# Starting TensorE's operands at multiples of 512 bytes in a four-layer decoder trunk

## The chip, the core and the metric

The kernel runs on one core of one Trainium2 chip. The metric is the device time of one execution in microseconds (us); of several executions the median is taken.

## What is computed

A trunk of four layers on 256 tokens of width 1024, all in 32-bit floating point. Each layer is a token mixer and a multilayer perceptron (MLP), both on the RMS-normalised input, both added to it:

```
for i in range(DEPTH):
    h = _rms_norm(x, attn_norm[i])
    ...
    x = x + y.astype(x.dtype)
    hm = _rms_norm(x, mlp_norm[i])
    x = x + jnp.square(jax.nn.relu(hm @ mlp_w_up[i])) @ mlp_w_down[i]
```

The mixers `y` are, in order: sparse attention with compressed, selected and windowed keys; stick-breaking attention; a convolution module; and block attention. The MLP widens 1024 to 4096 and back. Every mixer begins and ends with a large product with a weight matrix, too.

## The kernel before

Every large product is made three times in a split form: an operand `a` is written as `hi + lo`, `hi` being `a` rounded to the type float32r, which TensorE takes in one pass, and the product is `hi*hi + hi*lo + lo*hi`. A weight tile `raw` comes from memory by a DMA of SyncE, ScalarE rounds it into `wh` (L157), VectorE writes the rest into `wl` (L158). Activations are split the same way into `xT` (normalised input), `oT` (output of a mixer) and, in the MLP, `u`.

A matrix product on TensorE has a stationary operand (at most 128 columns, loaded by a LDWEIGHTS instruction ahead of it) and a moving operand (up to 512 columns streamed through). Five groups of products make up nearly all the work:

- `dn` (L190 to L192, called for the MLP's down projection): stationary `u`, moving `wh` or `wl`, 512 columns;
- `projT` (L211, the MLP's up projection): stationary `wh` (512 columns moving) or `wl` (256), moving `xT`;
- `proj` (L190 to L192, projections of the mixers): stationary `xT`, moving `wh` or `wl`, 512 columns, some 384 or 280;
- `acc` (L218 to L220, out projections): stationary `wh` or `wl`, moving `oT`, 256 columns;
- `ab` (L917, the convolution's input projection): stationary `wh` or `wl`, moving `xT`, 256 columns.

An MLP runs eight steps j: the up projection of 512 hidden columns, their squared ReLU into `u`, and, a step behind, the down projection of the step before. A step has 64 products `projT` and 48 products `dn`. "Stages 0 to 3" below are the MLPs of the four layers; stage 1 runs inside a pool `taps` that holds tiles of the convolution to come.

Memory is given out by pools, each a run of tiles one behind the other in the order of first use, at steps of 32 bytes: `const` first (`xr`, the residual stream, then small tables), then `rawp` (three `raw`), `hlp` (eight `wh`, eight `wl`), `act` (`xT`, `oT` and helpers), `sm` (small statistics), and behind them a pool for each stage, `mlp0` with `s`, `b`, `q`, `u` for instance. So the length of an early tile sets where all later ones begin, and most tiles have lengths that are multiples of 512 bytes.

Of the kernel before, what the change touches and what calls it, by code (L numbers as in the profile page):

```python
# [10 lines left out]
F32 = mybir.dt.float32  # L11
F32R = mybir.dt.float32r
# [4 lines left out]
P = 128  # L17
# [50 lines left out]
def trunk(ctx: ExitStack, tc: tile.TileContext, A: dict, out: bass.AP):  # L68
    nc = tc.nc
    const = ctx.enter_context(tc.tile_pool(name="const", bufs=1))  # L70
    rawp = ctx.enter_context(tc.tile_pool(name="rawp", bufs=3))
    hlp = ctx.enter_context(tc.tile_pool(name="hlp", bufs=8))
    act = ctx.enter_context(tc.tile_pool(name="act", bufs=2))
    sm = ctx.enter_context(tc.tile_pool(name="sm", bufs=4))
    ps = ctx.enter_context(tc.tile_pool(name="ps", bufs=2, space=bass.MemoryType.PSUM))

    def bank(tag, name):
        return ps.tile([P, 512], F32, tag=tag, bufs=4 if tag == "B" else 2, name=name)
# [732 lines left out]
    def taps_tile(ch):  # L811


        w = tapp.tile([P, 8, 4, 32], F32, tag="taps", bufs=4, name="taps")
        nc.vector.tensor_tensor(w.rearrange("p g m (e q) -> p (g m e) q", q=16),
                                eye[:, None, :].to_broadcast([P, 64, 16]),
                                tp[:, ch, :, None].to_broadcast([P, 64, 16]), op=ALU.mult)
        taps[ch] = w
# [160 lines left out]
    def moba(n):  # L979
# [114 lines left out]
                o.go(range(4, 8), range(8))  # L1094
        return nxt

    xr = const.tile([P, KT, S], F32, name="xr")
    gains = const.tile([P, 8, KT], F32, name="gains")
    ident = const.tile([P, P], F32, name="ident")
    nc.scalar.dma_start(gains, A["norms"])  # L1100
    nc.scalar.dma_start(ident, A["ident"])
    nhalf = const.tile([P, 4], F32, name="nhalf")
    nc.vector.memset(nhalf, -0.5)
    mean = const.tile([P, P], F32, name="mean")
    nc.vector.memset(mean, 1.0 / D)
    n = start_norm(0)
    feats = list(range(KT))
# [11 lines left out]
    for _ in range(10):  # L1119
        nc.tensor.matmul(o[:, :P], lhsT=mean, rhs=mean, start=True, stop=True)  # L1120

    identr = const.tile([P, P], F32R, name="identr")
    n = nsa(n, load_x)
    n = mlp(0, n, 1)
    n = stick(n)
# [1 line left out]
    with tc.tile_pool(name="taps", bufs=1) as tapp:  # L1127
        tp = tapp.tile([P, KT, 64], F32, name="tp")
        nc.sync.dma_start(tp, A["conv_taps"])
        eye = tapp.tile([P, 16], F32, name="eye")  # L1130
        nc.sync.dma_start(eye, A["eye16"])
        n = mlp(1, n, 2, lambda j: taps_tile(j) if j < 4 else None)
        n, raw = conv(n)
# [123 lines left out]
```

## Time and profile before

| | |
|---|---|
| time, median of 3 runs | 1180.42 us (1180.06 to 1180.87) |
| profiled execution, its own time | 1180.44 us |
| its span (first to last instruction) | 1178.7 us |
| TensorE busy | 1167.1 us, 99% |
| TensorE weight loads | 1008.7 us, 86% |
| VectorE busy | 782.9 us, 66% |
| ScalarE busy | 620.9 us, 53% |
| DMA engines, share busy by hardware queue q1 | 47.0% |

TensorE's products overlap one another, so a product's duration is longer than its share of the time; the distance from the start of one to the start of the next is what counts. A weight load lies beside the product before it.

The rows of a stretch read: its limits and length in us, then busy us and count of TensorE, its weight loads, VectorE, ScalarE (and GpSimd where it appears), then TensorE's granted clock as a share of 2.4 GHz, the busy share of the DMA engines and what they moved in GB/s. Busy time there is the time covered, overlaps counted once.

### The profile page before, as it was taken

Reading aid. Unit: us, or ns where it says so; the run is one execution under the profiler, and the core shown is the slowest. Engines: PE = TensorE matmul, PEld = TensorE weight load, DVE = VectorE, ACT = ScalarE, POOL = GpSimd, SP = SyncE. Lnnn points to the kernel's source line nnn. Section 1 sums busy time; section 2 is a strip of 40 time slices with the busy share of each in tenths; the row PEclk is TensorE's granted clock in tenths of the full one; section 3 lists DMA queues with packets and bytes.
Section 4 is the critical chain, followed back from the end, with each engine's and each line's share of the span. In section 5 each row is a group of like instructions: output and inputs, shape, how many; then the busy total and the mean of one; then the engine's idle time right before and its main releaser. Section 6 shows DMA issues by size and latency. Waiting matters only on the chain.

```text
span 1178.7 us, 17661 instructions
## 1 busy us (share of the span) xinstructions
PE 1167.1 (99%) x7046; PEld 1008.7 (86%) x7046; DVE 782.9 (66%) x1206; ACT 620.9 (53%) x1031; POOL 33.2 (3%) x50
## 2 busy tenths in 40 slices
PE   9999999999999999999999999999999999999998
PEld 6798988888888998888889998888888889888886
DVE  7788675656585686656665677656659886656553
ACT  6487554444565654544563275454446665544441
POOL 1100000000000000000001100000001100000000
PEclk9999999999999999999999999999999999999999
DMA  8554255545454436545545746455455543555440
GB/s 303 203 186 144 77 210 214 185 172 204 154 201 163 144 129 222 190 183 198 188 151 165 251 172 222 164 197 212 153 195 178 182 162 118 187 214 192 165 178 36
DMA packets 35650, 211.11 MB, mean 179 GB/s; under 512 B 4592, under 2 KB 7664, under 8 KB 12016
## 3 DMA queue, kind: packets, MB, share of 16 engines
q1 hardware_dynamic: 31104, 198.76, 47.0%
q0 software_dynamic: 1568, 6.80, 2.1%
q10 hardware_dynamic: 2896, 4.42, 1.1%
q8 instruction: 55, 0.90, 0.3%
q14 instruction: 27, 0.22, 0.1%
HBM read 207.74 MB, written 2.23 MB: 178 GB/s over the span
## 4 chain that ended last, share of the span: by engine, by line
PE 67%; issue 26%; DVE 3%; ACT 2%; DMA 1%; POOL 1%; SPq 0%; POOLq 0%; ACTq 0%; DVEq 0%
PE projT L211 23%; PE dn L190 8%; PE dn L192 8%; PE dn L191 8%; PE ab L917 2%; PE proj L192 2%; PE proj L191 2%; PE proj L190 2%; PE acc L218 2%; PE acc L220 2%; PE acc L219 2%; DVE wl L158 1%; PE po L675 1%; ACT wh L157 1%; PE cv L859 1%
## 5 line engine op out<-in xcount | busy, mean ns | idle before, releaser
L158 DVE TENSOR_TENSOR wl<-raw,wh 128x1024 fp32r<-128x1024 f32 (+1 forms) x372 | 441.1, 1212 | 186.9 <-ACT wh L157 182.8
L157 ACT CAST wh<-raw 128x1024 fp32r<-128x1024 f32 (+1 forms) x372 | 376.1, 1041 | 215.6 <-PE dn L192 111.2
L211 PE MATMUL projT<-xT,wh 128*128 128x512 f32 x1152 | 361.5, 396 | 0.3 <-DVE xT L101 0.3
L211 PEld LDWEIGHTS projT<-xT,wl 128*128 128x128 f32 x1152 | 215.3, 188 | 49.9
L211 PE MATMUL projT<-xT,wl 128*128 128x256 f32 x1152 | 225.4, 278 | 0.0
L190 PE MATMUL dn<-wh,u 128*128 128x512 f32 x512 | 202.7, 396 | 0.0
L192 PE MATMUL dn<-wh,u 128*128 128x512 f32 x512 | 202.0, 395 | 0.0
L191 PE MATMUL dn<-wl,u 128*128 128x512 f32 x512 | 201.4, 393 | 0.0
L211 PEld LDWEIGHTS projT<-xT,wh 128*128 128x128 f32 x1152 | 178.2, 189 | 3.7 <-DVE xT L101 0.5
L192 PEld LDWEIGHTS dn<-wh,u 128*128 128x128 f32 x512 | 96.4, 188 | 22.4
L191 PEld LDWEIGHTS dn<-wl,u 128*128 128x128 f32 x512 | 96.4, 188 | 20.7
L190 PEld LDWEIGHTS dn<-wh,u 128*128 128x128 f32 x512 | 96.5, 188 | 20.4
L316 ACT COPY b<-projT 128x256 f32<-128x256 f32 x128 | 41.2, 374 | 93.7 <-PE projT L211 93.4
L191 PE MATMUL proj<-wl,xT 128*128 128x512 f32 (+2 forms) x224 | 85.9, 384 | 2.5 <-DVE wl L158 2.1
L190 PE MATMUL proj<-wh,xT 128*128 128x512 f32 (+2 forms) x224 | 85.7, 385 | 0.4 <-ACT wh L165 0.3
L317 DVE TENSOR_TENSOR s<-projT,b 128x256 f32<-128x256 f32 x128 | 48.2, 418 | 55.0 <-ACT b L316 55.0
L192 PE MATMUL proj<-wh,xT 128*128 128x512 f32 (+2 forms) x224 | 84.5, 378 | 0.0
L89 ACT CAST u<-q 128x1024 fp32r<-128x1024 f32 x32 | 33.6, 1049 | 82.9 <-DVE q L319 82.7
L218 PE MATMUL acc<-oT,wh 128*128 128x256 f32 x256 | 73.8, 292 | 0.0
L219 PE MATMUL acc<-oT,wh 128*128 128x256 f32 x256 | 72.7, 285 | 0.0
L220 PE MATMUL acc<-oT,wl 128*128 128x256 f32 x256 | 71.2, 284 | 0.0
L90 DVE TENSOR_TENSOR u<-q,u 128x1024 fp32r<-128x1024 f32 x32 | 39.2, 1226 | 34.5 <-ACT u L89 34.5
(231 smaller groups left out, 1252.6 us busy)
## 6 DMA issues: line engine op xcount, KB each, us to landing
raw<-in_down SPq DMA_DIRECT2D x64, 1024.0 KB, 4.8
raw<-in_up SPq DMA_DIRECT2D x63, 1024.0 KB, 4.8
raw<-in_sb_w SPq DMA_DIRECT2D x12, 1024.0 KB, 4.8
raw<-in_moba_w SPq DMA_DIRECT2D x12, 1024.0 KB, 4.9
raw<-in_conv_w SPq DMA_DIRECT2D x8, 1024.0 KB, 4.7
st<-dr POOLq DMA_DIRECT2D x16, 287.0 KB, 6.3
raw<-in_nsa_w SPq DMA_DIRECT2D x4, 1024.0 KB, 5.9
rawc<-in_nsa_cmp SPq DMA_DIRECT2D x4, 1024.0 KB, 4.8
```

The lines of the kernel that those rows point to most:

```text
L90: return a, nc.vector.tensor_sub(lo, src, hi.bitcast(F32))
L157: nc.scalar.copy(wh[:, :w], r)
L158: nc.vector.tensor_sub(wl[:, :w], r, wh[:, :w].bitcast(F32))
L190: nc.tensor.matmul(o, lhsT=aT[:, kt, 0, t, :], rhs=wh, start=first, stop=False)
L191: nc.tensor.matmul(o, lhsT=aT[:, kt, 0, t, :], rhs=wl, start=False, stop=False)
L192: nc.tensor.matmul(o, lhsT=aT[:, kt, 1, t, :], rhs=wh, start=False, stop=last)
L211: nc.tensor.matmul(o[:, :width], lhsT=v[kt][part][:, f * P:(f + 1) * P], rhs=rhs, start=kt == 0 and part == 0, stop=kt == KT - 1 and part ...
L218: nc.tensor.matmul(o, lhsT=wh, rhs=aT[:, kt, 0], start=first, stop=False, skip_group_check=True)
L219: nc.tensor.matmul(o, lhsT=wh, rhs=aT[:, kt, 1], start=False, stop=False, skip_group_check=True)
L220: nc.tensor.matmul(o, lhsT=wl, rhs=aT[:, kt, 0], start=False, stop=last, skip_group_check=True)
L316: nc.scalar.copy(b, o[:, S:])
L317: nc.vector.tensor_add(s[:, f], o[:, :S], b)
```

## The change

Tiles of the pool `const` are put in another order, and four tiles are added or widened only to fill space: `front` (384 bytes) ahead of `xr`, `nhalf` from 4 to 64 columns, `back` (384 bytes, in a pool of its own behind `sm`), and `eye` from 64 to 512 bytes, of which the first 64 are used. `front` and `back` are never read or written. The memset of `nhalf` covers its new width. No other instruction differs, and on each engine the instructions stand in the same order with the same waits.

```diff
     sm = ctx.enter_context(tc.tile_pool(name="sm", bufs=4))
+    edge = ctx.enter_context(tc.tile_pool(name="edge", bufs=1))
     ps = ctx.enter_context(tc.tile_pool(name="ps", bufs=2, space=bass.MemoryType.PSUM))
+    edge.tile([P, 96], F32, name="back")
...
+    const.tile([P, 96], F32, name="front")
     xr = const.tile([P, KT, S], F32, name="xr")
+    ident = const.tile([P, P], F32, name="ident")
+    identr = const.tile([P, P], F32R, name="identr")
+    mean = const.tile([P, P], F32, name="mean")
     gains = const.tile([P, 8, KT], F32, name="gains")
-    ident = const.tile([P, P], F32, name="ident")
...
-    nhalf = const.tile([P, 4], F32, name="nhalf")
+    nhalf = const.tile([P, 64], F32, name="nhalf")
     nc.vector.memset(nhalf, -0.5)
-    mean = const.tile([P, P], F32, name="mean")
     nc.vector.memset(mean, 1.0 / D)
...
-    identr = const.tile([P, P], F32R, name="identr")
...
-        eye = tapp.tile([P, 16], F32, name="eye")
+        eye = tapp.tile([P, P], F32, name="eye")[:, :16]
```

Where tiles begin in a partition's memory, as the remainder of the byte address by 512:

| tile | before | after |
|---|---|---|
| `xr` | 128 | 0 |
| `ident` | 384 | 0 |
| `identr`, `mean` | 416 | 0 |
| `raw`, `wh`, `wl` (all buffers) | 416 | 0 |
| `xT`, `oT` (all buffers) | 416 | 0 |
| `u` in stages 0, 2 and 3 | 32 | 0 |
| `u` in stage 1 (behind the pool `taps`) | 96 | 0 |
| `y` (stages 0 and 2; stage 1) | 32; 96 | 0; 0 |
| attention's `kT`, `vv` | 32 | 0 |
| convolution's `taps`, `st` | 96, 448 | 0, 352 |

Within `xT`, `oT` and `u`, and within `wh` and `wl` at widths of 512 and 1024 columns, every operand of a large product begins a multiple of 512 bytes behind the tile's start; at the width of 280 columns (1120 bytes) every second one does not.

## Rows read from the trace of the kernel before

**Rows 1.** The page's engine table: busy time, share of the span, instructions.

```profile
PE 1167.1 (99%) x7046; PEld 1008.7 (86%) x7046; DVE 782.9 (66%) x1206; ACT 620.9 (53%) x1031; POOL 33.2 (3%) x50
```

**Rows 2.** The page's chain that ended last, by engine and by line.

```profile
PE 67%; issue 26%; DVE 3%; ACT 2%; DMA 1%; POOL 1%; SPq 0%; POOLq 0%; ACTq 0%; DVEq 0%
```

**Rows 3.** TensorE's products by shape: count, busy us, mean ns, idle before.

```profile
L211 PE MATMUL projT<-xT,wh 128*128 128x512 f32 x1152 | 361.5, 396 | 0.3 <-DVE xT L101 0.3
L211 PE MATMUL projT<-xT,wl 128*128 128x256 f32 x1152 | 225.4, 278 | 0.0
L190 PE MATMUL dn<-wh,u 128*128 128x512 f32 x512 | 202.7, 396 | 0.0
...
L218 PE MATMUL acc<-oT,wh 128*128 128x256 f32 x256 | 73.8, 292 | 0.0
...
L190 PE MATMUL proj<-wh,xT 128*128 128x512 f32 x176 | 69.6, 398 | 0.4 <-ACT wh L165 0.3
...
L917 PE MATMUL ab<-xT,wh 128*128 128x256 f32 x256 | 47.1, 285 | 0.0
L917 PE MATMUL ab<-xT,wl 128*128 128x256 f32 x128 | 36.2, 283 | 0.0
```

**Rows 4.** Stretches with one `dn` block each, its instructions alone; stages 0, 1, 3.

```profile
186.90:198.40 11.50, 11.32 (x48) 8.90 (x48) 0.00 (x0) 0.00 (x0) 1.00 0.50 184
...
475.50:487.00 11.50, 11.16 (x48) 8.85 (x48) 0.00 (x0) 0.00 (x0) 1.00 0.51 182
...
1040.70:1052.20 11.50, 11.32 (x48) 8.94 (x48) 0.00 (x0) 0.00 (x0) 1.00 0.51 184
```

**Rows 5.** TensorE's timeline (start, duration): 47 `proj` products, first and last.

```profile
906.34 0.39 PE L191 MATMUL proj<-wl,xT 128*128 128x512 f32 x1
...
916.79 0.39 PE L192 MATMUL proj<-wh,xT 128*128 128x512 f32 x1
```

**Rows 6.** TensorE's timeline: 139 `ab` products, first and last.

```profile
629.75 0.28 PE L917 MATMUL ab<-xT,wl 128*128 128x256 f32 x1
...
646.29 0.28 PE L917 MATMUL ab<-xT,wl 128*128 128x256 f32 x1
```

**Rows 7.** A stretch that holds one step of `projT`, its instructions alone.

```profile
175.80:186.94 11.14, 11.13 (x64) 9.68 (x63) 0.76 (x2) 0.65 (x2) 1.00 0.51 188
```

**Rows 8.** Timeline of TensorE: every sixth product of 280 columns.

```profile
45.09 0.29 PE L190 MATMUL proj<-wh,xT 128*128 128x280 f32 x1
...
45.86 0.29 PE L190 MATMUL proj<-wh,xT 128*128 128x280 f32 x1
...
46.63 0.29 PE L190 MATMUL proj<-wh,xT 128*128 128x280 f32 x1
```

**Rows 9.** Timeline of TensorE: two neighbouring products of `dn`.

```profile
187.41 0.40 PE L192 MATMUL dn<-wh,u 128*128 128x512 f32 x1
187.65 0.40 PE L190 MATMUL dn<-wh,u 128*128 128x512 f32 x1
```

**Rows 10.** Two transposes' weight loads by tile: least, median, most ns; starts.

```profile
L285 PEld LDWEIGHTS xt<-ident,xr x16: 139/140/224, 1016.6 to 1019.4; 128*128 128x128 f32 x16
...
L297 PEld LDWEIGHTS yT<-ident,y x48: 138/140/143, 314.9 to 886.7; 128*128 128x128 f32 x48
```

**Rows 11.** The start: VectorE's memset by group, TensorE's timeline.

```profile
L1105 DVE MEMSET mean<- 128x128 f32 x1 | 0.2, 165 | 0.0
...
1.09 4.18 PE L1120 MATMUL warm<-mean 128*128 128x128 f32 x20 [1.09 <-DVE mean L1105]
5.56 0.73 PE L190 MATMUL proj<-wh,xT 128*128 128x512 f32 x2 [0.30 <-ACT wh L165]
```

**Rows 12.** All engines in stretches of rows 5 and 4 (stages 0, 1).

```profile
906.33:916.80 10.47, 10.47 (x48) 8.64 (x47) 10.47 (x16) 6.13 (x8) 2.01 (x2) 1.00 0.37 133
...
186.90:198.40 11.50, 11.50 (x52) 9.34 (x52) 6.38 (x7) 4.83 (x7) 0.00 (x0) 1.00 0.50 184
475.50:487.00 11.50, 11.50 (x53) 9.44 (x52) 6.51 (x8) 4.97 (x7) 0.00 (x0) 1.00 0.51 182
```

## The prediction

> **What bounds the kernel now.** The engine table comes first [rows 1]: TensorE is busy 1167.1 us of a span of 1178.7, the next engine (VectorE) 782.9. The chain of waits [rows 2] agrees: PE 67% plus "issue" 26% (time in which TensorE waited for nothing the profile shows), 3% for VectorE, 1% for DMA. So the time is the number of matrix products times the pace at which they start, and the change, which alters only where tiles lie, can reach the time through that pace alone.
>
> The pace is not the duration in the groups. There all 512-column products read 396 to 398 ns [rows 3], but neighbours overlap. The pace is read from start to start. In [rows 5] 47 products of 512 columns by `proj` start between 906.34 and 916.79: 46 intervals in 10.45 us, 227.2 ns each. In [rows 6] 139 products of 256 columns by the convolution start between 629.75 and 646.29: 138 intervals in 16.54 us, 119.9 ns each. Between them a column costs (227.2 - 119.9) / 256 = 0.419 ns, which is one column per cycle of the 2.4 GHz level (the granted clock is 1.00 in every stretch shown [rows 4]), and some 13 ns per product are left that no column pays for.
>
> The `dn` products (down projections) are slower at the same width. A block of 48 occupies 11.32 us in stages 0 and 3 and 11.16 us in stage 1 [rows 4]; less one duration of 0.395, over 47 intervals, that is 232.5 and 229.0 ns. So 5.3 and 1.8 ns above `proj`. What differs? Not what runs beside: the two stages show the same company [rows 12], VectorE 6.38 and 6.51 us of 11.50, ScalarE 4.83 and 4.97, DMA share 0.50 and 0.51; and the quicker `proj` stretch has VectorE busy all through. What does differ is the table of starts above: in `proj` both operands start at 416 within 512 bytes; in `dn` the moving one (`wh`, `wl`) starts at 416 and the stationary one (`u`) at 32 in stages 0, 2 and 3, and at 96 in stage 1. The pace follows the distance of the two starts (0, 128, 192 bytes within 512). I read this as the weight load of the next product and the stream of the running one meeting in memory, more or less often by their distance.
>
> The Trainium skill speaks against that ("TensorE: Matmul & The Clock Gate", section "Step-by-step: what each phase is for"): TensorE has two independent read ports, and loading the next weights takes nothing from the running matmul. By that rule placement would be free and the sum nothing, 1180.4 us; the two stages of [rows 4] differ all the same, so the trace does not bear it out here. No mechanism is proved by two placements, and the rule's result stays a rival.
>
> **The change part by part.**
>
> The program's instructions, their order and their waits are the same; one memset is wider, and addresses move.
>
> *The `dn` products.* `u` now starts at 0 within 512, as `wh` and `wl` do, so their distance is 0, as it always was in `proj`. If the pace follows the distance, `dn` goes to 227.2 ns: 3 stages x 384 x (232.5 - 227.2) = 6.1 us, and 384 x (229.0 - 227.2) = 0.7 us, together 6.8 us. Bounds: nothing, if distance is not the cause; and on the other side the slowest single interval that `dn` shows, 0.24 us [rows 9], as the pace of all: 1152 x (240 - 232.5) + 384 x (240 - 229.0) = 12.9 us lost. I take 227.2, since `proj` runs the same sequence (three products per weight pair, the same `wh` and `wl` buffers, a stationary tile of the same layout) at the distance that `dn` gets.
>
> *All other large products.* `projT` (weights stationary, `xT` moving), `proj`, `acc` and `ab` have both operands at 416 before and at 0 after: the distance stays 0 and only the absolute start moves. No row shows one of them at a multiple of 512 with both operands, so the price is bounded. Two rows speak for nothing. In the products of 280 columns the moving operand starts at 416 in six products and, one row of the weight tile further (1120 bytes), at 0 in the next six: starting at 45.09, 45.86 and 46.63 [rows 8], so 0.77 us for six either way, though the distance shifts with it. And the 128-column transposes load weights in a median 140 ns whether the stationary tile is `xr` (at 128, 512 bytes a slice) or `y` (at 32 or 96) [rows 10]. The bound for a gain is the whole 13 ns: 5,520 products in the groups of [rows 3] (1152 + 1152, then 3 x 512, 3 x 256, 3 x 176, 256 + 128) x 13 = 72 us. For a loss it is what a bad placement has cost `dn`, 5.3 ns on the 3,984 others: 21 us. I take 0.
>
> `projT` keeps its own small excess: 64 products in 11.13 us [rows 7], less one duration of 0.278 and over 63 intervals, is 172.2 ns, where the mean of 227.2 and 119.9 is 173.6; the last product is a short one, so it is at the level of the others within 1 ns. Nothing to win there by distance.
>
> *Other engines.* VectorE, ScalarE and the DMA queues see the same shapes at other addresses. All are covered: TensorE is the bound, and a gain of 6.8 us lowers the cover by 0.6%. If that cover failed, the next late thing would be `wl` in `dn` (VectorE, 782.9 us busy), far off.
>
> *The memset.* `nhalf` grows from 4 to 64 columns. The 128 columns of `mean` behind it take 165 ns [rows 11], so the growth costs between 0 and 0.17 us on VectorE. Behind it wait `mean` and the ten warming products, which end at 1.09 + 4.18 = 5.27 us; the first real product waits until 5.56 for ScalarE's `wh` [rows 11]. The delay is inside those 0.3 us; without that cover it would cost some 0.08 by columns. I take 0.
>
> *Sum.* The profiled execution took 1180.44 us, 0.02 above the median of the three runs, 1180.42. 1180.44 - 6.8 = 1173.6 us.
>
> **The rivals.** About 0.2% (2.4 us) is what a measurement of this kernel can tell from no change; on the 1,536 `dn` products that is 1.5 ns each, on all 5,520 0.43 ns.
>
> A, the forecast: `dn` goes to the pace of `proj`. With 227 to 231 ns reached, 1170 to 1178. For it: two placements, two paces, the same in each of the 48-product blocks [rows 4]. Chance 0.47.
>
> B, nothing moves: `dn` is slow for a reason of its own (it waits less often than `proj`, so its weight loads come at another moment), and placement only nudges it. The time stays within 1178.1 to 1182.8. Against it: `proj` has the same order. Chance 0.22.
>
> C, the absolute start matters to all products, since a start off some boundary makes the array fetch one piece more. Then the 13 ns go in part or whole: half of them on 5,520 is 36 us, which gives 1144; all 72, 1108; a tenth on top of A, 1166. The same page of the Trainium skill (section "Back-to-back issue gap") gives N / 2.4 + 2.5 ns for an isolated gap, by which 512 columns would take 215.8 and not the 227.2 measured; that leaves room for C, and no run here shows such a pace. For C: nothing large in this trace is aligned, so nothing refutes it. Against: [rows 8, 10]. Chance 0.16, 0.10 of it below 1160.
>
> D, slower: the distance of 0 suits `proj` by its walk over the tiles, not `dn`; the weight load and the stream now begin at the same place and meet at every product. Place: `dn`, in all four stages. If `dn` goes to its 0.24 us level throughout, 1180.4 + 12.9 = 1193; it decides from a mean pace of (1152 x 232.5 + 384 x 229.0) / 1536 = 231.6 ns upward, and shows as slower from 233.1. For it: single `dn` intervals at that level exist. Chance 0.15.
>
> **How the numbers follow.** The time is A's, 1173.6. Faster: A and C, 0.63; same: B, 0.22; slower: D, 0.15. The range takes A, B, the lower edge of D (up to 1184) and the part of C above 1160: 0.47 + 0.22 + 0.04 + 0.06 = 0.79. A alone is 1170 to 1178.
>
> **What would show it.** In the changed kernel's trace 48 `dn` products should occupy 0.395 + 47 x 0.2272 = 11.07 us in every stage, stage 1 no longer apart from the rest; `proj`, `ab` and `projT` should keep 227, 120 and 11.13 us. If `proj` and `ab` are quicker, C is right; if `dn` keeps 11.32 and 11.16, B; if a `dn` block takes over 11.4 us, D. The forecast is wrong if distance is not the cause, or if absolute starts count.

## The result and the profile after

The changed kernel takes 1172.55 us (median of 5, 1171.66 to 1173.2) against 1180.06 beside it: a ratio of 0.9935, 95% interval 0.9921 to 0.995. The forecast was 1173.6. The changed file is longer ahead of the products, so their lines move by two: `dn` and `proj` are now L192 to L194, `projT` L213, `acc` L220 to L222, `ab` L919.

The groups of TensorE's products by shape answer to [rows 3]:

```profile
L213 PE MATMUL projT<-xT,wh 128*128 128x512 f32 x1152 | 361.4, 396 | 0.3 <-DVE xT L103 0.3
L213 PE MATMUL projT<-xT,wl 128*128 128x256 f32 x1152 | 225.3, 278 | 0.0
L192 PE MATMUL dn<-wh,u 128*128 128x512 f32 x512 | 200.3, 391 | 0.0
```

Even in these overlapping durations `dn` alone has moved, from 396 to 391 ns. The pace shows in the stretches with one block of 48 `dn` products (its instructions alone; stages 0, 1 and 3), which answer to [rows 4]:

```profile
185.60:197.10 11.50, 11.05 (x48) 8.87 (x48) 0.00 (x0) 0.00 (x0) 1.00 0.51 184
472.30:483.80 11.50, 11.05 (x48) 8.84 (x48) 0.00 (x0) 0.00 (x0) 1.00 0.52 182
1033.90:1045.40 11.50, 11.05 (x48) 8.84 (x48) 0.00 (x0) 0.00 (x0) 1.00 0.53 184
```

All three are 11.05 us, where [rows 4] had 11.32, 11.16 and 11.32: stage 1 no longer stands apart. Less one duration of 0.39, over 47 intervals, that is 226.8 ns. Of the full blocks only the first of stages 0 to 2 is slower, before as after: its first interval takes 0.31 to 0.32 us, and it occupies 11.17 us, where before had 11.40 in stages 0 and 2 and 11.24 in stage 1. The same 47 `proj` products as in [rows 5] and the same 139 `ab` products as in [rows 6], first and last of each on TensorE's timeline:

```profile
899.82 0.39 PE L193 MATMUL proj<-wl,xT 128*128 128x512 f32 x1
...
910.27 0.39 PE L194 MATMUL proj<-wh,xT 128*128 128x512 f32 x1
```

```profile
625.78 0.28 PE L919 MATMUL ab<-xT,wl 128*128 128x256 f32 x1
...
642.32 0.28 PE L919 MATMUL ab<-xT,wl 128*128 128x256 f32 x1
```

10.45 us over 46 intervals and 16.54 over 138 are the very figures of before. So starting at a multiple of 512 bytes gave `proj` and `ab` nothing in these stretches. Added up over all `dn` products, the times from each start to the next start on TensorE fall from 356.6 to 349.7 us: 6.9 us of the 7.5 between the medians.

### The profile page after: what moved, and what is told of

Same layout as the page of the kernel before. It is cut to its first block, busy times and chain, and to the rows that moved or that the text cites. A ratio compares the mean times of both kernels' runs of the same rounds, so it can differ in the third digit from the quotient of the medians.

```text
span 1169.9 us, 17661 instructions
## 1 busy us (share of the span) xinstructions
PE 1159.5 (99%) x7046; PEld 1008.0 (86%) x7046; DVE 782.7 (67%) x1206; ACT 621.2 (53%) x1031; POOL 34.3 (3%) x50
## 4 chain that ended last, share of the span: by engine, by line
PE 67%; issue 26%; DVE 3%; ACT 2%; DMA 1%; POOL 1%; ACTq 0%; POOLq 0%; DVEq 0%
PE projT L213 23%; PE dn L192 7%; PE dn L194 7%; PE dn L193 7%; PE ab L919 2%; PE proj L194 2%; PE proj L193 2%; PE proj L192 2%; PE acc L220 2%; PE acc L222 2%; PE acc L221 2%; PE po L677 1%; DVE wl L160 1%; PE cv L861 1%; ACT wh L159 1%
## 5 line engine op out<-in xcount | busy, mean ns | idle before, releaser
L213 PE MATMUL projT<-xT,wh 128*128 128x512 f32 x1152 | 361.4, 396 | 0.3 <-DVE xT L103 0.3
L213 PEld LDWEIGHTS projT<-xT,wl 128*128 128x128 f32 x1152 | 215.2, 188 | 49.8
L213 PE MATMUL projT<-xT,wl 128*128 128x256 f32 x1152 | 225.3, 278 | 0.0
L192 PE MATMUL dn<-wh,u 128*128 128x512 f32 x512 | 200.3, 391 | 0.0
L194 PE MATMUL dn<-wh,u 128*128 128x512 f32 x512 | 199.5, 390 | 0.0
L213 PEld LDWEIGHTS projT<-xT,wh 128*128 128x128 f32 x1152 | 178.2, 189 | 3.5 <-DVE xT L103 0.5
L194 PEld LDWEIGHTS dn<-wh,u 128*128 128x128 f32 x512 | 96.1, 188 | 20.2
L192 PEld LDWEIGHTS dn<-wh,u 128*128 128x128 f32 x512 | 96.1, 188 | 18.7
L192 PE MATMUL proj<-wh,xT 128*128 128x512 f32 (+2 forms) x224 | 85.6, 384 | 0.4 <-ACT wh L167 0.4
L194 PE MATMUL proj<-wh,xT 128*128 128x512 f32 (+2 forms) x224 | 84.4, 377 | 0.0
L220 PE MATMUL acc<-oT,wh 128*128 128x256 f32 x256 | 74.0, 293 | 0.0
L222 PE MATMUL acc<-oT,wl 128*128 128x256 f32 x256 | 71.1, 284 | 0.0
```

Source lines behind the costliest of these rows:

```text
L192: nc.tensor.matmul(o, lhsT=aT[:, kt, 0, t, :], rhs=wh, start=first, stop=False)
L194: nc.tensor.matmul(o, lhsT=aT[:, kt, 1, t, :], rhs=wh, start=False, stop=last)
L213: nc.tensor.matmul(o[:, :width], lhsT=v[kt][part][:, f * P:(f + 1) * P], rhs=rhs, start=kt == 0 and part == 0, stop=kt == KT - 1 and part ...
L220: nc.tensor.matmul(o, lhsT=wh, rhs=aT[:, kt, 0], start=first, stop=False, skip_group_check=True)
L222: nc.tensor.matmul(o, lhsT=wl, rhs=aT[:, kt, 0], start=False, stop=last, skip_group_check=True)
```

## Experiments

"Distance" is the start of the stationary operand less that of the moving one. Distance theory: the pace depends on it. Absolute theory: it depends on whether an operand starts on a boundary.

**Distance against absolute start.** In the kernel before, `u` alone is moved inside a wider tile (the diff); in the second run, in the changed kernel, the same edit with 32, 48, 32 and 32 elements brings back the old distances.

```diff
-                u = mp.tile([P, 4, 2, NT, P], F32R, tag="u", name="u")
+                uw = mp.tile([P, 2048 + 128], F32R, tag="u", name="u")
+                at = (96, 80, 96, 96)[i]
+                u = uw[:, at:at + 2048].rearrange("p (f a t c) -> p f a t c", f=4, a=2, t=NT)
```

> The kernel before, with u alone moved inside a wider tile so that it begins at 416 within 512 bytes in all four stages, as the weight tiles do. Distance 0, no operand at a multiple of 512. Distance theory: a block of 48 dn products falls from 11.32 and 11.16 us to 11.06, the time to about 1173 us, as with the whole change. Absolute theory (a start on a boundary counts): nothing is on a boundary, blocks and time stay as before, 1180 us.

Measured: 1172.51 us, 0.994 (0.9928 to 0.9953) of before: the whole gain, with none of the change's lines. `dn` blocks of stages 0 and 1:

```profile
186.00:197.50 11.50, 11.05 (x48) 8.89 (x48) 0.00 (x0) 0.00 (x0) 1.00 0.50 184
472.70:484.20 11.50, 11.05 (x48) 8.91 (x48) 0.00 (x0) 0.00 (x0) 1.00 0.50 182
```

> The changed kernel, with u alone moved to 128 (stages 0, 2, 3) and 192 (stage 1) within 512 bytes, the distances to the weight tiles that the kernel before had; all else stays at multiples of 512. Distance theory: blocks of dn return to 11.32 us in stages 0, 2, 3 and 11.16 in stage 1, the time to 1180 us. Absolute theory with a boundary of 64 bytes or less: u is still on it, blocks stay at 11.06 us and the time at 1172.5; with a boundary of 128, stages 0, 2, 3 stay at 11.06 and stage 1 alone becomes slower.

Measured: 1179.03 us, 0.9997 (0.9988 to 1.0006) of before. The gain is gone, although the weight tiles start at a multiple of 512 and `u` at one of 64. `dn` blocks of stages 0 and 1 are those of [rows 4] again:

```profile
186.20:197.70 11.50, 11.32 (x48) 8.92 (x48) 0.00 (x0) 0.00 (x0) 1.00 0.50 184
474.70:486.20 11.50, 11.16 (x48) 8.91 (x48) 0.00 (x0) 0.00 (x0) 1.00 0.49 182
```

Together the two runs settle it for `dn`: distance 0 is enough, and aligned starts without it are worth nothing.

**How the pace depends on the distance.** The changed kernel, with the same edit and another distance in each stage. The third run was chosen after the first two had been read.

> The changed kernel with u at a distance of 64, 256, 320 and 384 bytes from the weight tiles in stages 0, 1, 2 and 3. Distance theory: each stage has its own pace, the same in all its blocks, between 226.9 and about 233 ns (blocks of 11.06 to 11.35 us), none quicker than at distance 0. Absolute theory: 256 bytes and 384 bytes at the pace of distance 0, 64 and 320 slower.

> The changed kernel with u at a distance of 16, 32, 160 and 448 bytes from the weight tiles in stages 0, 1, 2 and 3. Distance theory: small distances (16, 32) stay near 226.9 ns, 160 lies between the known 232.5 at 128 and 229.0 at 192, 448 near 227 to 229. Absolute theory (boundary of 64 bytes): 16, 32 and 160 slower by the same amount, 448 at 226.9.

> The changed kernel with u at a distance of 208, 224, 240 and 96 bytes from the weight tiles in stages 0 to 3. So far 0 and 256 gave 226.9 ns, 16, 32, 64, 160 and 320 gave 233.3 to 233.4, 128 and 384 gave 232.5, 192 and 448 gave 229.1: the distance counts within 256 bytes. Distance theory: 96 near 233, 208 to 240 between 229 and 233. If a distance just short of 256 lets the weight load run clear of the stream, one of 208 to 240 falls below 226.9; I expect none.

Measured, one execution each, 1179.23 and 1180.86 us; `dn` blocks of stages 0 to 3, at 64, 256, 320, 384 bytes, then at 16, 32, 160, 448:

```profile
186.00:197.60 11.60, 11.37 (x48) 8.87 (x48) 0.00 (x0) 0.00 (x0) 1.00 0.50 182
474.80:486.30 11.50, 11.05 (x48) 8.91 (x48) 0.00 (x0) 0.00 (x0) 1.00 0.49 182
748.80:760.40 11.60, 11.37 (x48) 8.89 (x48) 0.00 (x0) 0.00 (x0) 1.00 0.49 181
1039.50:1051.00 11.50, 11.31 (x48) 8.93 (x48) 0.00 (x0) 0.00 (x0) 1.00 0.51 184
```

```profile
186.60:198.20 11.60, 11.36 (x48) 8.97 (x48) 0.00 (x0) 0.00 (x0) 1.00 0.50 182
475.70:487.20 11.50, 11.36 (x48) 8.87 (x48) 0.00 (x0) 0.00 (x0) 1.00 0.50 182
751.80:763.30 11.50, 11.36 (x48) 8.87 (x48) 0.00 (x0) 0.00 (x0) 1.00 0.50 182
1042.20:1053.70 11.50, 11.16 (x48) 8.89 (x48) 0.00 (x0) 0.00 (x0) 1.00 0.50 184
```

256 equals 0, 320 equals 64, 384 equals 128 (11.31 and 11.32) and 448 equals 192: to within 0.01 us the pace repeats every 256 bytes. The absolute theory in the forms set down above fails again: 384 and 448, on boundaries of 128 and 64 bytes, are slower than 256. (With everything else at 0 these runs can't exclude a boundary of 256; the first experiment did, with `u` and the weight tiles all at 416.) My own guess that 16 and 32 bytes stay near 226.9 ns was wrong, too: 16 bytes already cost 0.31 us a block. The third run, 1180.44 us, at 208, 224, 240 (two blocks of stage 2, one in each of `u`'s two buffers) and 96:

```profile
186.20:197.70 11.50, 11.29 (x48) 8.93 (x48) 0.00 (x0) 0.00 (x0) 1.00 0.52 184
474.80:486.40 11.60, 11.36 (x48) 8.91 (x48) 0.00 (x0) 0.00 (x0) 1.00 0.50 181
751.30:762.80 11.50, 11.05 (x48) 8.90 (x48) 0.00 (x0) 0.00 (x0) 1.00 0.51 182
773.30:784.80 11.50, 11.13 (x48) 8.92 (x48) 0.00 (x0) 0.00 (x0) 1.00 0.52 182
1040.20:1051.70 11.50, 11.40 (x48) 8.89 (x48) 0.00 (x0) 0.00 (x0) 1.00 0.53 184
```

No distance beats 0, and 96 is the worst. At 240 the two buffers differ by 0.08 us, in turn from block to block, so the remainder within 256 bytes is not the whole rule.

**Do the other products depend on it?** `xT` and `oT` are moved by the same kind of edit, a distance for each layer.

> The changed kernel with xT moved away from the weight tiles (u stays at distance 0): stationary less moving start is, within 256 bytes, 192, 128, 64 and 16 for projT in stages 0 to 3, 128 for proj in layer 1 (stick-breaking), 64 for proj in layer 3 (block attention) and 128 for ab. If the distance counts for every product of this kind: proj rises from 227 to about 232.5 and 233.4, four products of projT from 697 ns to over 700 in some stages, ab from 120 up; the time rises by 3 to 12 us over 1172.5. If it counts for dn's sequence only, proj, projT and ab stay, and so does the time.

> As the run before with other distances: 240, 224, 160 and 32 for projT in stages 0 to 3, 192 for proj in layer 1, 240 for proj in layer 3, 192 for ab. If the distance counts for every product: proj at 192 goes to about 229 ns, projT differs from stage to stage by up to 4% of its 697 ns. If for dn only, all stay.

Measured: 1172.26 and 1174.23 us, one execution each. Mean ns from start to start, without those that a wait stretched (for `projT`, of four products in a row, two of 512 and two of 256 columns). Each figure comes from one layer or stage of one trace:

| distance within 256 | 0 | 16 | 32 | 64 | 128 | 160 | 192 | 224 | 240 |
|---|---|---|---|---|---|---|---|---|---|
| `proj` | 228.2 | | | 233.3 | 232.7 | | 229.8 | | 228.1 |
| `projT`, four | 696.3 | 698.0 | 702.8 | 693.9 | 697.7 | 706.5 | 691.5 | 694.2 | 696.8 |
| `ab` | 119.9 | | | | 118.6 | | 117.2 | | |
| `acc` | 119.6 | 117.4 | 118.3 | 115.9 | 119.3 | 119.9 | 115.3 | 117.6 | 117.2 |

`proj` at 512 columns behaves as `dn` does. At 280 columns nothing of the kind shows: the two groups of six in [rows 8] lie at distances 0 and 160 and take 0.77 us each, while 160 costs `dn` 6.5 ns a product, which would be 0.04 us in six. `projT`, whose stationary operand is the weight tile, is quickest at 192 and not at 0; the kernel with a distance for each group, below, puts all four stages at 192, and each takes 691.6 to 692 ns.

For `ab` and `acc`, the other two with the weight tile stationary, the table says less than it seems to. At distance 0 `acc` keeps to 119.3 to 120.0 ns in every layer of nine traces. At 64 and 192 it runs at one of two levels, for many products on end. Layer 0 of the first of these runs and of the kernel with a distance for each group has the same code and the same places up to here. The same 91 products of `acc`, first and last, in the one and then in the other:

```profile
127.16 0.28 PE L222 MATMUL acc<-oT,wh 128*128 128x256 f32 x1
...
137.36 0.28 PE L222 MATMUL acc<-oT,wh 128*128 128x256 f32 x1
```

```profile
127.19 0.28 PE L222 MATMUL acc<-oT,wh 128*128 128x256 f32 x1
...
137.79 0.28 PE L222 MATMUL acc<-oT,wh 128*128 128x256 f32 x1
```

Over 90 intervals that is 113.3 and 117.8 ns. So a mean such as 115.3 is a mixture of the two levels, and the columns of `acc` at 64 and 192 can't be ranked by it. Both levels are below what distance 0 gives. `ab` has the same two: at 192 its means were 117.2, 115.6, 115.6 and 117.8 in four traces.

The 3 to 12 us lost that I expected for the first of these runs did not come: `acc`, `ab` and `projT` gave back what `proj` lost.

**Which product pays.** `u`'s rounded part and its rest get separate distances.

> The changed kernel with u's rounded part and its rest at different distances from the weight tiles: 0 and 64 bytes in stage 0, 64 and 0 in stage 1, 0 and 128 in stage 2, 0 and 0 in stage 3. The three products of dn are rounded part on wh, rounded part on wl, rest on wh. If the stream meets the weight load of the next product: in stage 0 the second product is slow (about 233 ns) and the others 226.9; in stage 1 the first and third are slow. If it meets its own weights: in stage 0 the third is slow, in stage 1 the first and second. Stage 3, a changed layout at distance 0, stays at 226.9.

Measured, `dn` blocks of stages 0 to 3:

```profile
186.20:197.70 11.50, 11.27 (x48) 8.85 (x48) 0.00 (x0) 0.00 (x0) 1.00 0.52 184
474.50:486.00 11.50, 11.37 (x48) 8.89 (x48) 0.00 (x0) 0.00 (x0) 1.00 0.50 182
751.20:762.70 11.50, 11.27 (x48) 8.91 (x48) 0.00 (x0) 0.00 (x0) 1.00 0.51 182
1040.80:1052.30 11.50, 11.05 (x48) 8.89 (x48) 0.00 (x0) 0.00 (x0) 1.00 0.52 184
```

The control, stage 3, is as expected. But in stage 0 the three products take a mean of 229.5, 230.1 and 234.3 ns: the one with the displaced weights pays most, the others pay too. In stage 1 they take 232.9, 232.0 and 234.1, all slow; in stage 2, 227.8, 232.5 and 233.8. Neither expectation holds; the run is inconclusive about which product is stretched.

**A distance for each group.** The last line stands for `oT` in all four mixers.

```diff
-        n.xT = act.tile([P, KT, 2, NT, P], F32R, tag="aT", name="xT")
+        at = (0, 0, 16, 0, 16, 16, 16, 16)[i]
+        n.xT = act.tile([P, 4096 + 128], F32R, tag="aT", name="xT")[:, at:at + 4096].rearrange("p (k a t c) -> p k a t c", k=KT, a=2, t=NT)
...
-            oT = act.tile([P, KT, 2, NT, P], F32R, tag="aT", name="oT")
+            oT = act.tile([P, 4096 + 128], F32R, tag="aT", name="oT")[:, 16:16 + 4096].rearrange("p (k a t c) -> p k a t c", k=KT, a=2, t=NT)
```

> The changed kernel with a distance for each group of products: u at 0 and xT of the attention layers at 0 as changed; xT of the four MLPs and of the convolution layer, and oT, at 64 bytes, so that projT, ab and acc have weight tile less activation at 192 within 256 bytes, the quickest measured for each (four projT 691.5 against 696.3 ns, ab 117.2 against 119.9, acc 115.3 against 119.6). Distance theory: 512 x 4.8 + 384 x 2.7 + 768 x 4.3 ns = 6.8 us less than the changed kernel's 1172.5, 1165.7 us. Theory that a multiple of 512 is best for all: nothing gained, 1172 us or more.

Measured: 1168.55 us, 0.9906 (0.989 to 0.9923) of before. The direction holds, the size does not: 4.0 us below the changed kernel's 1172.55 and not 6.8. `acc` reached 117.4 ns in the mean and not the 115.3 that one layer had shown, since here it ran mostly at the upper of its two levels. The run was repeated beside the changed kernel, with a variant:

> The changed kernel itself, as a neighbour on the same chip for the two runs beside it. 1172.5 us, 0.9935 of the kernel before.

> The kernel with a distance for each group (xT of the MLPs and of the convolution layer, and oT, at 64 bytes) a second time, beside the changed kernel. From its trace: projT 2.3 us, ab 1.6, acc 0.9 less than the changed kernel, 4.8 together: 1167.7 us. If a multiple of 512 is as good, 1172.5.

> The same with oT at 192 bytes, so that acc alone has the distance 64 within 256 bytes and not 192. If the distance alone sets the pace, all four layers' acc go to the 115.9 ns that one layer showed at 64, from 117.4: 768 x 1.5 ns, 1.1 us less than the run beside it. If the layer counts as well, they differ from one another and the time stays within 0.5 us.

Measured: 1172.69 us, 0.9939 (0.9926 to 0.9951), for the changed kernel; 1168.21, 0.9902 (0.9888 to 0.9915), and 1168.03, 0.9898 (0.9883 to 0.9913), for the other two. So 4.5 us more can be had, and the version beats both kernels. The variant's time is no different: its `acc` gained in two layers (117.0, 117.5, 114.0, 114.7 ns) while its `ab`, whose operands had not been moved, went from 115.6 to 117.8. Distance is not all that sets these two groups. A step of 64 `projT` products, stage 0, in the changed kernel and in the version with a distance for each group:

```profile
196.50:207.90 11.40, 11.30 (x64) 9.68 (x63) 0.76 (x2) 0.65 (x2) 1.00 0.49 184
```

```profile
196.50:207.90 11.40, 11.24 (x64) 9.68 (x64) 0.75 (x2) 0.65 (x2) 1.00 0.50 184
```

## Why the prediction was right, and where it was not

**The main term.** "`dn` goes to 227.2 ns", 6.8 us: measured 226.8 to 226.9 in every full block but the first of each stage (229.4), and 6.9 us in the sum. The reason, distance rather than absolute start, rested on two placements of `u`; the two runs that took one without the other showed it. That the distance counts only within 256 bytes, and that most others are slower than the two known ones, the prediction did not have. The sentence of the Trainium skill ("TensorE: Matmul & The Clock Gate", section "Step-by-step: what each phase is for") that loading the next tile's weights takes no bandwidth from the running matmul does not make placement free in this kernel: the first experiment differs from before in `u`'s place and its padding, and is 6.9 us quicker.

**"All other large products": 0.** Right for this change: `proj` and `ab` kept 227.2 and 119.9 ns with their distance at 0 and their absolute start moved. But [rows 8], which the prediction took as a sign against the absolute start, is no sign for distance either: there the distance moved by 160 and the pace did not.

**`projT`: "nothing to win there by distance".** Wrong, and by a misreading: the stretch of [rows 7] ends at 186.94, inside the last product, so 11.13 us is cut short. The whole step is 11.30 us before as after, 175.0 ns a product and above the 173.6 of the mean; at 192 bytes it is 11.24. In the version with a distance for each group the whole of `projT` takes 2.4 us less than in the changed kernel. For the forecast the error cost nothing, since the change leaves `projT`'s distance alone.

**The memset.** Predicted 0 to 0.17 us, hidden. The memset of `nhalf` now takes 112 ns, 50 more than before, and TensorE's first work starts at 1.13 us instead of 1.09 [rows 11]. The first real product still waits for ScalarE's `wh`, 0.38 us.

```profile
L1109 DVE MEMSET nhalf<- 128x64 f32 x1 | 0.1, 112 | 0.8 <-PEq L1250 0.8
...
1.13 4.36 PE L1125 MATMUL warm<-mean 128*128 128x128 f32 x20 [1.13 <-DVE mean L1110]
5.87 0.50 PE L192 MATMUL proj<-wh,xT 128*128 128x512 f32 x1 [0.38 <-ACT wh L167]
```

**The profiled executions.** They differ by 1180.44 - 1171.66 = 8.8 us, 1.9 more than `dn`'s sum. 1.1 of it is gained before the first `dn` product, which starts at 163.50 instead of 164.57. In the runs that moved only `u` in the changed kernel, so with the same first layer, it starts between 163.63 and 164.27, and in the changed kernel run again at 164.27. So most of this goes from execution to execution and is not the change's.

**The rivals.** B (a reason of `dn`'s own) and C (absolute start) fall with the first pair of experiments. D (slower) did not come at distance 0, but places of its kind exist: at 96 bytes a block takes 11.40 us, 234 ns, past the 233.1 from which D would have shown. The 240 ns of its price appeared as the pace of no block of 48. (Nor are they the slowest single interval, as the prediction has it: a stage's first one takes 0.31 to 0.32 us; 0.24 is the slowest inside a block.)

**What stays open.** That the weight load of one product and the stream of another meet in memory was my reading of the mechanism; it is argued, not shown. The run with `u`'s parts at separate distances contradicts its simple form. Why `projT` has another best distance, and what decides between the two levels of `ab` and `acc`, is unknown.

## What to carry to other kernels

Read TensorE's pace from start to start, by group of products and by stage; two stages that run the same code at different paces beside the same company point at addresses. Then move one operand at a time against the other within 256 bytes: padding everything to round addresses is not needed, and is not the best for every group. Read a gain in more than one layer and trace before counting on it: one layer's 115.3 ns did not come back. A tile inserted early in a pool can shift this distance for all later stages unnoticed.

## What the runs showed that was not expected

- The pace of `dn` repeats every 256 bytes of distance (11.05 us a block at 0 and 256, 11.37 at 64 and 320), and 16 bytes off 0 cost as much as 160 (11.36).
- The 13 ns per product above one column per cycle are not fixed: at distances of 64 and 192 `acc`, with 256 columns, runs for long at 113.3 or at 117.8 ns, where it takes 119.3 to 120.0 at 0. The same code at the same places showed either level.
- At the same remainder within 256 bytes (240), `u`'s two buffers gave 11.05 and 11.13 us.
